# The output projection of a decoder block, as eight block products or as seven

## The chip, the cores and the metric

The kernel runs on one core of a Trainium2 chip. Such a core has several engines with instruction queues of their own: TensorE multiplies matrices (a weight load holds one operand still, the other streams through), VectorE and ScalarE do elementwise work, and GpSimd (POOL) and SyncE (SP) here mostly issue transfers. TensorE's results go to PSUM, eight banks of 512 float32 columns in 128 partitions. The metric is the device time of one execution in microseconds (us), as the median of several runs.

## The reference

The reference is one layer: two token mixers side by side, merged by gates, then an output projection, then an MLP with a squared ReLU. The sequence is 512 tokens, the width 1024, the MLP's inner width 4096, all in float32. What matters here is its end:

```
glu = g_s @ w_glu[l] + b_glu[l]
y_ssm = glu[..., :D_MODEL] * jax.nn.sigmoid(glu[..., D_MODEL:])

mixed = jax.nn.sigmoid(z_gla) * y_gla + jax.nn.sigmoid(z_ssm) * y_ssm
h = h + rmsnorm(mixed @ w_out[l], g_mix_post[l])

hn = rmsnorm(h, g_ffn_pre[l])
f = jnp.square(jax.nn.relu(hn @ w_ff1[l])) @ w_ff2[l]
h = h + rmsnorm(f, g_ffn_post[l])
```

`rmsnorm(x, g)` is x times the reciprocal root of the mean of its squares, times g.

## The kernel before

Every dense product is made in three passes. A float32 operand is split into a high half, rounded by a ScalarE copy to the reduced type that TensorE takes (`split_hi`, L160), and a low half, which VectorE makes by subtracting the high half (L175, L1428, L1444). The product is the sum of high x high, high x low and low x high, so one block of 128 x 128 weights against up to 512 columns costs three matmuls.

The stages that the change touches follow one another:

- The GLU (from L1398). Its 16 output tiles of 128 channels by 512 tokens are made in four groups of 256 channels: first the two sigmoid tiles of a group, then its two value tiles. A tile is 8 blocks x 3 passes = 24 matmuls. When a value tile is complete, VectorE adds the bias and multiplies by the gate (L1425), adds the other mixer's part (L1426) and the result, `mixed` in the reference, is split into `mh` and `ml`. The weights come over the SP queue into `wraw`, with three buffers.
- The output projection (`w_out_passes`, `h_rows`). All of w_out is loaded and split ahead, into `woh` and `wol`. Then the four tiles of 128 token rows follow one another, each with two banks of 512 output channels and 48 matmuls.
- The rows (`h_rows`). For each row tile: squares (ScalarE) and multiplication by `gpost`, a root (`row_scale`, a handful of operations on one column), addition of x (L1491), squares and multiplication by `gffn` (L1493), another root, and scaling to `hn` (L1496 on VectorE, L1497 on ScalarE). A row tile is then turned by eight TensorE transposes into two banks (L66), and one ScalarE and one VectorE operation per bank split it into `hh` and `hl`. The turn of row tiles 0 and 1 stands two row tiles after they are made, that of 2 and 3 among the first MLP tiles.
- The first MLP matrix (ff1). Three tiles (`EARLY`) first run on the columns of row tiles 0 and 1 alone, and later on the columns of 2 and 3. The others use all 512 columns at once.
- The second MLP matrix is already made as one level of Strassen's algorithm, from L1580 on, with its own sums of blocks.

TensorE's instructions keep their written order through these stages. VectorE's and ScalarE's are ordered by a planner, which goes by its own estimate of when an instruction could run and, among those that could, takes the one written first; `issue_after` queues a part behind a given instruction of the same engine. On the chip each engine then works off its queue in that order. A tile's tag has a number of buffers, and whoever wants the next one waits until it is free.

Of the kernel before, what the change touches and what calls it, by code (L numbers as in the profile page):

```python
# [10 lines left out]
F32R = mybir.dt.float32r  # L11
# [39 lines left out]
def hybrid_block(ctx: ExitStack, tc: tile.TileContext, io, out: bass.AP):  # L51
# [43 lines left out]
    def f32(t):  # L95
        return t.bitcast(F32)
# [26 lines left out]
    G.memset(sgn[:64], 1.0)  # L123
    G.memset(sgn[64:], -1.0)

    vecs = mk(cst, [P, 36], tag="vecs")
    V_GN, V_BGLU, V_BGATE, V_D = 0, 8, 24, 28

    def bank(tag="sm"):
        return mk(ps_mm if tag == "mm" else ps_sm, [P, 512], tag=tag)  # L130
# [28 lines left out]
    def split_hi(dst, src, scale=1.0):  # L159
        S.activation(dst, src, AF.Copy, scale=scale)  # L160
# [21 lines left out]
    def load_w(src):  # L182

        return [split_w(raw_w(src[:, c : c + P])[1]) for c in range(0, src.shape[1], P)]
# [1202 lines left out]
    s1.close()  # L1387


    sw = ExitStack()  # L1390
    pw = pool("pw", stack=sw, padded=True)
    mh = mk(pw, [P, KT, SEQ], F32R, tag="mh")
    ml = mk(pw, [P, KT, SEQ], F32R, tag="ml")
# [4 lines left out]
    for m in range(KT):  # L1398
        if m == NBLK - 1:
            q = blocks[m].qT  # L1400
        else:
            q = mk(pgl, [P, SEQ], tag="qi", bufs=4)
            nc.gpsimd.dma_start(q, qd[m])
        split_hi(gh[:, m], q)
        V.tensor_sub(gl[:, m], q, f32(gh)[:, m])
    wg = io["w_glu"][0]
    for c in range(0, D, 256):
        ss_ = []
        for i, w in enumerate(load_w(wg[:, D + c : D + c + 256])):
            m = c // P + i  # L1410
            ps = bank("mm")
            feat_tile(w, gh, gl, 0, SEQ, ps)
            s_ = mk(pgl, [P, SEQ], tag="ms", bufs=2)
            S.activation(s_, ps, AF.Sigmoid, bias=vecs[:, V_BGLU + 8 + m : V_BGLU + 9 + m])
            zt = mk(pgl, [P, SEQ], tag="zi", bufs=2)
            nc.sync.dma_start(zt, zs[m])
            V.tensor_mul(s_, s_, zt)
            ss_.append(s_)
        for i, w in enumerate(load_w(wg[:, c : c + 256])):
# [6 lines left out]
            V.tensor_add(ss_[i], ss_[i], t)  # L1426
            split_hi(mh[:, m], ss_[i])
            V.tensor_sub(ml[:, m], ss_[i], f32(mh)[:, m])  # L1428
    sgl.close()
    skept.close()  # L1430


    h_dram = mk(dr, [TT, P, D], tag="hd")
    gpost = mk(pw, [P, D], tag="gpost")
    gffn = mk(pw, [P, D], tag="gffn")
    nc.scalar.dma_start(gpost, io["g_mix_post"][0].partition_broadcast(P))
    nc.scalar.dma_start(gffn, io["g_ffn_pre"][0].partition_broadcast(P))
    woh = mk(pw, [P, KT, D], F32R, tag="woh")
    wol = mk(pw, [P, KT, D], F32R, tag="wol")
    for k in range(KT):  # L1440
        raw = mk(wp, [P, D], tag="wraw", bufs=3)
        nc.sync.dma_start(raw, io["w_out"][0][k * P : (k + 1) * P, :])
        split_hi(woh[:, k], raw)
        V.tensor_sub(wol[:, k], raw, f32(woh)[:, k])  # L1444

    def squares(pl, acc, i, src):
        junk = mk(pl, [P, 512], tag="junk", bufs=2)
        S.activation(junk, src, AF.Square, accum_out=acc[:, i : i + 1])

    def sums(pl, tag):  # L1450
        return mk(pl, [P, 2], tag=tag + "acc", bufs=2)

    def row_scale(pl, acc, tag):

# [10 lines left out]
    def w_out_passes(t, pss, order):  # L1465

        ts_ = slice(t * P, (t + 1) * P)
        for k, n in order:
            ns = slice(n * 512, (n + 1) * 512)
            PE.matmul(pss[n], mh[:, k, ts_], woh[:, k, ns], start=(k == 0), stop=False)  # L1470
            PE.matmul(pss[n], mh[:, k, ts_], wol[:, k, ns], start=False, stop=False)
            PE.matmul(pss[n], ml[:, k, ts_], woh[:, k, ns], start=False, stop=(k == KT - 1))
            yield

    def h_rows(t, pss):

        xt = mk(pt, [P, D], tag="xt", bufs=2)
        for i in range(2):
            nc.sync.dma_start(xt[i * CH : (i + 1) * CH], io["x"][0].rearrange("(c t) d -> t c d", t=T8)[2 * t + i])
        acc = sums(pt, "wo")  # L1480
        ht = mk(pt, [P, D], tag="ht", bufs=2)
        for n in range(2):
            ns = slice(n * 512, (n + 1) * 512)
            squares(pt, acc, n, pss[n])
            V.tensor_mul(ht[:, ns], pss[n], gpost[:, ns])
        rs = row_scale(pt, acc, "wo")
        hn = mk(pt, [P, D], tag="hn", bufs=2)
        acc = sums(pt, "hn")
        for n in range(2):
            ns = slice(n * 512, (n + 1) * 512)  # L1490
            V.scalar_tensor_tensor(ht[:, ns], ht[:, ns], rs, xt[:, ns], op0=ALU.mult, op1=ALU.add)  # L1491
            squares(pt, acc, n, ht[:, ns])
            V.tensor_mul(hn[:, ns], ht[:, ns], gffn[:, ns])  # L1493
        nc.gpsimd.dma_start(h_dram[t], ht)
        rs = row_scale(pt, acc, "hn")
        V.tensor_scalar(hn[:, :512], hn[:, :512], rs, None, op0=ALU.mult)  # L1496
        S.activation(hn[:, 512:], hn[:, 512:], AF.Copy, scale=rs)  # L1497
        return hn

    hns = []  # L1500
    for t in range(TT):
        pss = [bank("mm") for _ in range(2)]
        order = [(k, n) for n in range(2) for k in range(KT)]
        if t == 0:
            order = [(k, n) for k in range(KT) for n in range(2)]
        for i, _ in enumerate(w_out_passes(t, pss, order)):
            if i == 2 and t >= 2:
                transpose_tokens(hns[t - 2], P, hh, hl, (t - 2) * P, "sm")
        hns.append(h_rows(t, pss))

    EARLY = 3
    w1 = io["w_ff1"][0]
    w2 = io["w_ff2"][0]
    ws = load_w(w1[:, : EARLY * P])
    pss = [bank("mm") for _ in ws]
    for i, (w, ps) in enumerate(zip(ws, pss)):
        within = None
        if i == EARLY - 1:
            within = (4, lambda: transpose_tokens(hns[3], P, hh, hl, 3 * P, "sm"))
        feat_tile(w, hh, hl, 0, 256, ps[:, :256], within=within)  # L1520
        if i == 0:
            transpose_tokens(hns[2], P, hh, hl, 2 * P, "sm")
    spt.close()
    sw.close()
    pff = pool("pff", padded=True)
# [2 lines left out]


    NJ = MF // 2  # L1530
    HT = SEQ // 2
    s1 = mk(pff, [P, NJ, HT], tag="s1")
    td2 = mk(dr, [4, NJ, P, 512], tag="t2d")

# [32 lines left out]
    pinned[0] = False  # L1567
    for m, ps in enumerate(pss):
        relu2(m, ps)
    j = 0  # L1570
    for m in range(EARLY, MF):
        ps = bank("mm")
# [128 lines left out]
def laid_out(np, given):  # L1701

    a = {name: np.asarray(given[name]) for name in _INS + _LAID}
    ar, ai, br, bi, cr, ci = (a[name][0] for name in ("a_re", "a_im", "b_re", "b_im", "c_re", "c_im"))
    step = np.broadcast_to(a["log_step"][0], (64, 64))
    rows = {"vecs": np.concatenate([a[n][0].reshape(-1, P) for n in ("gla_norm_g", "b_glu", "b_gate", "d_skip")]).T}
# [12 lines left out]

_LAID = ["g_mix_pre", "w_gate_up", "gla_norm_g", "b_glu", "b_gate", "d_skip", "a_re", "a_im", "log_step", "b_re", "b_im", "c_re", "c_im"]  # L1720
_INS = [
    "x", "meta_tokens", "w_in", "w_o_gla", "w_glu", "w_out", "g_mix_post", "g_ffn_pre", "w_ff1", "w_ff2", "g_ffn_post",
]
_OUTS = [((1, SEQ, D), "float32")]

# [18 lines left out]
```

## Time and profile before

| what | us |
|---|---|
| median of three runs | 875.36 (875.29 to 875.64) |
| the profiled execution | 874.97 |
| its span in the profile | 873.2 |
| GLU, first matmul to last | 403.0 to 490.1 |
| output projection, first matmul to last | 490.1 to 535.4 |
| first passes of three ff1 tiles, with two turns | 535.4 to 545.8 |

A timeline's or chain's row gives the start, the duration, engine and line, the operation, the output and inputs by name, their shapes and the count; in brackets stands the idle time before it and who ended it. A group's row gives the count, total busy time and, behind the comma, the mean in nanoseconds, then the idle time. A row of a table of stretches gives its bounds and length, then busy time and count for TensorE, its weight loads, VectorE, ScalarE and POOL, then TensorE's granted clock, the transfer engines' share and GB/s.

### The profile page before, as it was taken

To read this page: it belongs to the slowest core of one execution; us is meant where nothing else is said; L and a number is where in the kernel's file an instruction comes from. 1 tells how busy PE (TensorE), PEld (TensorE's weight loads), DVE (VectorE), ACT (ScalarE), POOL (GpSimd) and SP (SyncE) were. 2 spreads that over 40 slices of the span, in tenths; PEclk is the share of its full clock that TensorE was granted. 3 is DMA by queue.
4 is the path that set the end of the run, shared out by engine and by line. 5 is a ranking of instruction groups with operands and counts; after the bars stand their busy time and mean duration, and the time that the engine had idled before them with its cause. 6 is when DMAs were issued, how large, how long until landed. Compare 5 with 4: busy or idle time off the path is not lost.

```text
span 873.2 us, 13275 instructions
## 1 busy us (share of the span) xinstructions
PE 862.7 (99%) x4824; PEld 738.3 (85%) x4824; DVE 654.6 (75%) x1181; ACT 442.4 (51%) x749; POOL 121.4 (14%) x213
## 2 busy tenths in 40 slices
PE   9999999999999999999999999999999999999996
PEld 8998889898988888888888889888888888888884
DVE  7999889979686699855446656576766677688886
ACT  7677456676763554334333544333222236665763
POOL 1123021130303222241000001011111100000001
PEclk9999999999999999999999999999999999999999
DMA  9777766545455747658545842498989966755464
GB/s 315 235 228 230 209 140 162 168 137 158 113 145 160 242 133 208 209 151 298 155 147 174 238 132 100 142 352 291 320 289 341 320 224 232 272 195 198 169 199 140
DMA packets 166905, 180.57 MB, mean 207 GB/s; under 512 B 18056, under 2 KB 126760, under 8 KB 166840
## 3 DMA queue, kind: packets, MB, share of 16 engines
q1 hardware_dynamic: 146832, 115.95, 44.6%
q0 software_dynamic: 17744, 58.52, 19.8%
q10 hardware_dynamic: 2264, 5.25, 1.9%
q8 instruction: 38, 0.62, 0.3%
q14 instruction: 27, 0.22, 0.1%
HBM read 143.74 MB, written 35.95 MB: 206 GB/s over the span
## 4 chain that ended last, share of the span: by engine, by line
PE 95%; DVE 3%; ACT 1%; issue 0%; ACTq 0%; DVEq 0%
PE mm L61 70%; PE sm L61 23%; PE sm L66 2%; DVE wlo L79 1%; DVE M L79 0%; DVE c L1665 0%; ACT whi L79 0%; DVE xT L79 0%; ACTq L79 0%; ACT vs L79 0%; DVE vs L79 0%; DVE c L1659 0%; DVE d L79 0%; DVE mta L79 0%; ACT L79 0%
## 5 line engine op out<-in xcount | busy, mean ns | idle before, releaser
L160 ACT ACTIVATE whi<-wraw 128x1024 fp32r<-128x1024 f32 x82 | 86.9, 1059 | 210.6 <-PE mm L61 191.8
L175 DVE TENSOR_TENSOR wlo<-wraw,whi 128x1024 fp32r<-128x1024 f32 x82 | 100.3, 1223 | 98.2 <-ACT whi L160 98.0
L61 PE MATMUL mm<-xh,whi 128*128 128x512 f32 (+2 forms) x464 | 158.9, 342 | 0.0
L61 PE MATMUL mm<-xh,wlo 128*128 128x512 f32 (+2 forms) x464 | 155.9, 336 | 0.0
L61 PE MATMUL mm<-xl,whi 128*128 128x512 f32 (+2 forms) x464 | 155.6, 335 | 0.0
L61 PE MATMUL mm<-hh,whi 128*128 128x512 f32 (+1 forms) x280 | 104.0, 371 | 0.0
L61 PE MATMUL mm<-hl,whi 128*128 128x512 f32 (+1 forms) x280 | 103.8, 371 | 0.0
L61 PE MATMUL mm<-hh,wlo 128*128 128x512 f32 (+1 forms) x280 | 103.8, 371 | 0.0
L61 PEld LDWEIGHTS mm<-xh,whi 128*128 128x128 f32 x464 | 87.6, 189 | 9.5 <-issue 1.0
L61 PEld LDWEIGHTS mm<-xh,wlo 128*128 128x128 f32 x464 | 87.5, 189 | 9.0
L61 PEld LDWEIGHTS mm<-xl,whi 128*128 128x128 f32 x464 | 87.6, 189 | 8.4
L1602 DVE TENSOR_TENSOR wlo<-wraw,whi 128x1024 fp32r<-128x1024 f32 x56 | 68.4, 1223 | 20.1 <-ACT whi L1598 20.1
L61 PE MATMUL sm<-wlo,fh 128*128 128x512 f32 x192 | 74.8, 390 | 0.0
L61 PE MATMUL sm<-whi,fl 128*128 128x512 f32 x192 | 74.7, 389 | 0.0
L61 PE MATMUL sm<-whi,fh 128*128 128x512 f32 x192 | 74.7, 389 | 0.0
L1598 ACT ACTIVATE whi<-wraw 128x1024 fp32r<-128x1024 f32 x56 | 58.6, 1049 | 16.8 <-PE mm L61 11.7
L61 PEld LDWEIGHTS mm<-hh,whi 128*128 128x128 f32 x280 | 52.8, 188 | 9.1
L61 PEld LDWEIGHTS mm<-hh,wlo 128*128 128x128 f32 x280 | 52.7, 188 | 9.0
L61 PEld LDWEIGHTS mm<-hl,whi 128*128 128x128 f32 x280 | 52.8, 188 | 9.0
L160 ACT ACTIVATE fh<-f 128x512 fp32r<-128x512 f32 x48 | 30.3, 631 | 45.5 <-PE sm L61 30.3
L61 PE MATMUL mm<-gh,whi 128*128 128x512 f32 x128 | 49.8, 389 | 0.0
L61 PE MATMUL mm<-gl,whi 128*128 128x512 f32 x128 | 49.8, 389 | 0.0
(445 smaller groups left out, 1787.6 us busy)
## 6 DMA issues: line engine op xcount, KB each, us to landing
wraw<-in_w_ff_dram SPq DMA_DIRECT2D x56, 512.0 KB, 4.7
wraw<-in_w_in_dram SPq DMA_DIRECT2D x46, 512.0 KB, 4.1
w2raw<-in_w_ff_dram POOLq DMA_DIRECT2D x16, 1024.0 KB, 8.6
t2d<-w2t POOLq DMA_DIRECT2D x16, 1024.0 KB, 5.7
wraw<-t2d SPq DMA_DIRECT2D x32, 512.0 KB, 3.9
wraw<-in_w_glu_dram SPq DMA_DIRECT2D x16, 512.0 KB, 4.3
M<-kpad POOLq DMA_DIRECT2D x64, 64.0 KB, 3.1
wraw<-in_w_o_gla_dram SPq DMA_DIRECT2D x8, 512.0 KB, 6.1
```

The costliest lines, as they stand in the source:

```text
L61: ins = nc.tensor.matmul(*args, **kw)
L66: ins = nc.tensor.transpose(*args, **kw)
L79: return lambda *args, **kw: tc.keep_in_program_order(getattr(self.engine, name)(*args, **kw))
L160: S.activation(dst, src, AF.Copy, scale=scale)
L175: V.tensor_sub(lo, raw, f32(hi))
L1598: halved = S.activation(bh, raw, AF.Copy)
L1602: V.tensor_sub(bl, raw, f32(bh))
```

## The change

The 1024 x 1024 matrix w_out and the mixed rows are cut into 2 x 2 blocks: tokens in halves of 256, output channels in halves of 512, and the inner channels by even and odd tiles of 128. Instead of eight block products there are seven (Winograd's form of Strassen's algorithm), each of two row tiles by 4 inner blocks by 3 passes, of certain sums of the blocks:

- `mixed` makes the four sums of the mixed rows' blocks and splits all seven operands, as soon as a GLU tile is complete. It takes the place of the split into `mh` and `ml`.
- `out_load` and `out_weights` load two row blocks of w_out (1 MB) from the POOL queue in each of the four GLU groups, make four sums, split three of the seven weight operands, and store the other three sums in DRAM from the POOL queue. The buffer `woraw` is one. In the last group `out_weights` is queued behind the gating of its sigmoid tiles, in the others behind the addition of the value tiles.
- `later_b` reloads the four other weight operands (three sums, one block) over SP and splits them during the products, into the buffers of three earlier ones.
- The results are gathered from three pairs of banks. Row tiles 0 and 1 are complete after the fifth product, 2 and 3 after the seventh; each row tile's halves are squared and multiplied as they come.
- The MLP norm's vector `g_ffn_pre` no longer multiplies the rows (L1493 goes). It lies along partitions in `vecs` and is applied at the turn (`turn_rows`): eight ScalarE and eight VectorE operations of 128 columns for a row tile instead of two and two.
- Row 0 is turned inside the seventh product, row 1 right behind it, rows 2 and 3 among the first ff1 tiles. `EARLY` becomes 4; the fourth tile's weights go into a buffer pair of the projection's.

```diff
+    def out_load(j):
+        raw = mk(pwo, [P, 2, D], tag="woraw", bufs=1)
+        nc.gpsimd.dma_start(raw, w_out[2 * j * P : (2 * j + 2) * P, :].rearrange("(k p) n -> p k n", p=P))
+        return raw
+    def out_weights(j, raw):
+        w11, w12, w21, w22 = (raw[:, k, n : n + 512] for k in range(2) for n in (0, 512))
+        t1, t2, t3, t4 = (mk(pgl, [P, SEQ], tag="qi", bufs=4) for _ in range(4))
+        V.tensor_sub(t1, w12, w11)
+        V.tensor_sub(t2, w22, t1)
+        V.tensor_sub(t3, w22, w12)
+        V.tensor_sub(t4, w21, t2)
+        for (hi, lo), src in ((b1, w11), (b2_, w21), (b5_, t1)):
+            split_to(hi[:, j], lo[:, j], src)
+        for i, t in enumerate((t2, t3, t4)):
+            nc.gpsimd.dma_start(tdo[i, j], t)
+    def mixed(c, i, src):
+        m = src.rearrange("p (h t) -> p h t", h=2)
+        if i == 0:
+            split_to(ah[A11][:, c], al[A11][:, c], m[:, 0])
+            return
+        e, o = mixed.even, m
+        split_to(ah[A12][:, c], al[A12][:, c], o[:, 0])
+        split_to(ah[A22][:, c], al[A22][:, c], o[:, 1])
+        V.tensor_add(o[:, 1], e[:, 1], o[:, 1])
+        V.tensor_sub(e[:, 1], e[:, 0], e[:, 1])
+        V.tensor_sub(e[:, 0], o[:, 1], e[:, 0])
+        V.tensor_sub(o[:, 0], o[:, 0], e[:, 0])
+        for n, part in ((S1, o[:, 1]), (S2, e[:, 0]), (S4, o[:, 0]), (S3, e[:, 1])):
+            split_to(ah[n][:, c], al[n][:, c], part)
...
-            V.tensor_mul(hn[:, ns], ht[:, ns], gffn[:, ns])
...
+    def out_product(acc, i, b, t, first=False):
+        ts_ = slice(t * P, (t + 1) * P)
+        for k in range(4):
+            for n, (x_, w_) in enumerate(((ah[i], b[0]), (ah[i], b[1]), (al[i], b[0]))):
+                PE.matmul(acc[t], x_[:, k, ts_], w_[:, k], start=first and k == 0 and n == 0, stop=k == 3 and n == 2, skip_group_check=True)
+    def later_b(src):
+        hi, lo = b_slot()
+        for jj in range(2):
+            raw = mk(wp, [P, 2, 512], tag="wraw", bufs=3)
+            nc.sync.dma_start(raw, src(jj))
+            later_b.made = split_to(hi[:, 2 * jj : 2 * jj + 2], lo[:, 2 * jj : 2 * jj + 2], raw)
+        return hi, lo
...
+    def turn_rows(t):
+        col = slice(t * P, (t + 1) * P)
+        for q in range(2):
+            pv = turned_tokens(hns[t], P, q, "sm")
+            for k in range(4):
+                kk = 4 * q + k
+                g = vecs[:, V_GF + kk : V_GF + kk + 1]
+                S.activation(hh[:, kk, col], pv[:, k], AF.Copy, scale=g)
+                V.scalar_tensor_tensor(hl[:, kk, col], pv[:, k], g, f32(hh)[:, kk, col], op0=ALU.mult, op1=ALU.subtract)
...
+    for t in range(2):
+        out_product(Xo, A11, b1, t, True)
...
+    b6 = later_b(sums_of(0))
+    for t in range(2):
+        out_product(Zo, A12, b2_, t, True)
+        V.tensor_add(rows_[t][:, sides[0]], rows_[t][:, sides[0]], Zo[t])
+        out_half(t, 0, 0)
+        rows_x(t)
+    b3 = later_b(w22_of)
+    ws = load_w(w1[:, : 3 * P])
...
+        out_product(Yo, S1, b5_, t, True)
...
+    b7 = later_b(sums_of(1))
...
+        out_product(Xo, S2, b6, t)
+        S.copy(rows_[t][:, sides[1]], Xo[t])
+    b4 = later_b(sums_of(2))
+    for t in range(2):
+        out_product(Yo, S4, b3, t)
+        with tc.issue_after(later_b.made.ins):
+            V.tensor_add(rows_[t][:, sides[1]], rows_[t][:, sides[1]], Yo[t])
+        out_half(t, 1, 1)
+        hns[t] = h_rows(t)
...
+        out_product(Xo, S3, b7, t)
+        with tc.issue_after(out_half.squared.ins):
+            S.copy(rows_[2 + t][:, sides[1]], Xo[t])
...
+    for t in range(2):
+        out_product(Xo, A22, b4, t)
+        turn_rows(t)
+        out_half(2 + t, 0, 1, Xo[t])
+        hns[2 + t] = h_rows(2 + t)
+    EARLY = 4
...
+    with tc.issue_after(second[0].ins), tc.issue_after(second[1].ins):
+        split_to(*kept_w, raw)
...
+        within = (6, lambda: turn_rows(3)) if i == 2 else None
         feat_tile(w, hh, hl, 0, 256, ps[:, :256], within=within)
+        if i == 1:
+            turn_rows(2)
```

More of the change, by code (lines that the diff above doesn't have):

```diff
@@ L1405, in hybrid_block, with split_to @@
         V.tensor_sub(gl[:, m], q, f32(gh)[:, m])
+    def split_to(hi, lo, src):
+        split_hi(hi, src)
+        return V.tensor_sub(lo, src, f32(hi))
+    def out_load(j):
[27 more added lines that the diff above has]
+            split_to(ah[n][:, c], al[n][:, c], part)
     wg = io["w_glu"][0]
-    for c in range(0, D, 256):
+    for c4, c in enumerate(range(0, D, 256)):
         ss_ = []
@@ L1425, in hybrid_block, with sums @@
             V.scalar_tensor_tensor(ss_[i], ps, vecs[:, V_BGLU + m : V_BGLU + m + 1], ss_[i], op0=ALU.add, op1=ALU.mult)
-            V.tensor_add(ss_[i], ss_[i], t)
-            split_hi(mh[:, m], ss_[i])
-            V.tensor_sub(ml[:, m], ss_[i], f32(mh)[:, m])
+            added = V.tensor_add(ss_[i], ss_[i], t)
+            mixed.even = ss_[0].rearrange("p (h t) -> p h t", h=2)
+            mixed(c4, i, ss_[i])
+        if c4 < 3:
+            with tc.issue_after(added.ins):
+                out_weights(c4, raw)
     sgl.close()
+    swo.close()
     skept.close()
     h_dram = mk(dr, [TT, P, D], tag="hd")
[L1434 to L1444, printed above, removed]
     def squares(pl, acc, i, src):
         junk = mk(pl, [P, 512], tag="junk", bufs=2)
-        S.activation(junk, src, AF.Square, accum_out=acc[:, i : i + 1])
-    def sums(pl, tag):
-        return mk(pl, [P, 2], tag=tag + "acc", bufs=2)
+        return S.activation(junk, src, AF.Square, accum_out=acc[:, i : i + 1])
+    def sums(pl, tag, bufs=2):
+        return mk(pl, [P, 2], tag=tag + "acc", bufs=bufs)
     def row_scale(pl, acc, tag):
@@ L1478, in h_rows, with row_tile, rows_x @@
+    sides = slice(0, 512), slice(512, D)
+    accs = [sums(pt, "wo", 4) for _ in range(TT)]
+    xts_ = {}
+    def row_tile():
+        return f32(mk(pw, [P, 4, HT], F32R, tag="aq", bufs=14)).rearrange("p a b -> p (a b)")
+    def rows_x(t):
+        xt = xts_[t] = mk(pt, [P, D], tag="xt", bufs=2)
         for i in range(2):
             nc.sync.dma_start(xt[i * CH : (i + 1) * CH], io["x"][0].rearrange("(c t) d -> t c d", t=T8)[2 * t + i])
-        acc = sums(pt, "wo")
-        ht = mk(pt, [P, D], tag="ht", bufs=2)
@@ L1482, in h_rows, with out_half @@
[L1482 to L1486, printed above, removed]
+    def out_half(t, n, i, src=None):
+        dst = rows_[t][:, sides[n]]
+        src = dst if src is None else src
+        out_half.squared = squares(pt, accs[t], i, src)
+        V.tensor_mul(dst, src, gpost[:, sides[n]])
+    def h_rows(t):
+        ht, xt = rows_[t], xts_[t]
+        rs = row_scale(pt, accs[t], "wo")
```

95 lines of the change are left out of this document (55 added, 40 removed).

## The prediction

> **What bounds the kernel now.** I read the page's busy shares first, then the chain that ended last, then TensorE's own waits, then the busy time of the two stretches that the change touches (GLU 397.70 to 490.08, output projection to 535.60).
>
> ```profile
> PE 862.7 (99%) x4824; PEld 738.3 (85%) x4824; DVE 654.6 (75%) x1181; ACT 442.4 (51%) x749; POOL 121.4 (14%) x213
> ...
> PE 95%; DVE 3%; ACT 1%; issue 0%; ACTq 0%; DVEq 0%
> ```
> ```profile
> 397.71 116.33 PE mm L61 x513
> ...
> 539.33 4.31 PE mm L61 x36
> 543.63 0.87 PE sm L66 x8
> 544.50 167.85 PE mm L61 x780
> ```
> ```profile
> PE sm L61 <- DVE xss L513: 1.3, 1, 1.3
> PE sm L61 <- DVE xrs L79: 0.5, 1, 0.5
> PE sm L61 <- DVE meta L79: 0.3, 1, 0.3
> ```
> ```profile
> 397.70:490.08 92.38, 92.38 (x409) 76.43 (x408) 51.94 (x63) 37.37 (x46) 2.25 (x5) 1.00 0.60 193
> 490.08:535.60 45.52, 45.52 (x211) 37.87 (x210) 27.32 (x71) 19.51 (x44) 1.62 (x3) 1.00 0.49 139
> ```
>
> TensorE carries 95% of the chain. In both stretches the TensorE column fills the stretch, the clock is 1.00, and the only waits of TensorE that the trace shows (2.1 us) lie in other stages. So a matmul removed there is worth its full pitch, until something that it waits for comes late. VectorE has 40.4 us spare of 92.4 in the GLU and 18.2 of 45.5 in the projection; ScalarE has more.
>
> **The matmuls.** The pitch of a 512-column matmul is 116.33/513 = 0.2268 us, of a 256-column one 4.31/36 = 0.1197 us (the 0.39 us that single rows show overlap).
>
> ```profile
> L61 PE MATMUL mm<-woh,mh 128*128 128x512 f32 x64 | 25.1, 392 | 0.0
> ...
> L61 PE MATMUL mm<-woh,ml 128*128 128x512 f32 x64 | 24.9, 389 | 0.0
> L61 PE MATMUL mm<-wol,mh 128*128 128x512 f32 x64 | 24.9, 389 | 0.0
> ```
>
> Before: 3 x 64 = 192. After: 7 products x 2 row tiles x 4 blocks x 3 passes = 168, of the same shape. 24 x 0.2268 = 5.44 us less. EARLY from 3 to 4 splits one more ff1 tile: 48 x 0.1197 - 24 x 0.2268 = +0.30. The 32 transposes stay. Ceiling of the gain: 5.14 us. [...]
>
> **VectorE and ScalarE in the GLU.** Each step below starts from these prices; successive starts give the cost to the queue: 0.60 us for 512 columns, 1.14 for 1024. 256 columns: 0.42 less the same overlap of 0.08, 0.34.
>
> ```profile
> L1444 DVE TENSOR_TENSOR wol<-wraw,woh 128x1024 fp32r<-128x1024 f32 x8 | 9.8, 1224 | 3.3 <-ACT woh L160 3.1
> ...
> L1428 DVE TENSOR_TENSOR ml<-ms,mh 128x512 fp32r<-128x512 f32 x8 | 5.5, 688 | 0.1
> ...
> L1493 DVE TENSOR_TENSOR hn<-ht,gffn 128x512 f32<-128x512 f32 x8 | 5.1, 684 | 0.0
> ...
> L235 DVE TENSOR_TENSOR mta<-E 128x256 f32<-128x256 f32 x7 | 3.0, 422 | 0.0
> ```
> ```profile
> L160 ACT ACTIVATE whi<-wraw 128x1024 fp32r<-128x1024 f32 x82 | 86.9, 1059 | 210.6 <-PE mm L61 191.8
> ...
> L1642 ACT COPY c<-sm 128x512 f32<-128x512 f32 x6 | 3.5, 581 | 0.8 <-PE sm L61 0.8
> ```
> ```profile
> 474.88 1.22 DVE L175 TENSOR_TENSOR wlo<-wraw,whi 128x1024 fp32r<-128x1024 f32 x1 [1.82 <-ACT whi L160]
> 476.02 0.69 DVE L1417 TENSOR_TENSOR ms<-ms,zi 128x512 f32<-128x512 f32 x1
> ...
> 562.69 0.69 DVE L1554 TENSOR_TENSOR w2t<-w2raw 128x512 f32<-128x512 f32 x1
> 563.29 0.68 DVE L1543 TENSOR_TENSOR s<-f 128x512 f32<-128x512 f32 x1
> ```
>
> Per group of 256 columns the change adds `out_weights` (4 sums and 3 low halves, 7 x 0.60 = 4.2 us) and `mixed` (4 sums and 7 low halves, 11 x 0.34 = 3.7) and drops two low halves (1.2): +6.7 us on a group's 21.8, where VectorE now works 12.3 on average (51.94/92.38). It fits, so 0; if it did not, the matmul behind it would wait for its weights' low half. `wol` (9.8) leaves, but `later_b` brings 8 halves of the same price.
>
> **Queues.** SP loses 8 loads of w_out and gets 8 in `later_b`, behind the sums' stores. The ScalarE queue's gffn load goes, and gpost's now waits for memory of the GLU's tiles, with the splits of A12 and b6 queued behind it; these have 5 us of room each, so 0. POOL gets 4 loads and 12 stores; it was idle 98.63 us there, so only their landing counts.
>
> ```profile
> 506.02 0.54 POOL L1494 DMA_DIRECT2D hd<-ht  x1 [98.63 <-DVE ht L1491]
> ```
> ```profile
> 469.31 0.69 DVE L1426 TENSOR_TENSOR ms<-ms,ti 128x512 f32<-128x512 f32 x1
> ...
> 482.67 0.69 DVE L1417 TENSOR_TENSOR ms<-ms,zi 128x512 f32<-128x512 f32 x1
> ```
> ```profile
> DMA to landing us min/median/max: 6.3/8.6/10.0
> ```
>
> The place to watch is the last load, because `woraw` has one buffer. Group 2's `out_weights` may start after the addition at 469.31, and shares VectorE with `mixed` (3.4) and a weight split (1.1), so it ends near 479. Only then is the last megabyte loaded; the row above is that of the 1 MB loads of w_ff2 from the same queue, so it lands at 485 to 489, 488 by the median. Four sums (2.4), the low half of b1 (0.6), and the last but one GLU tile's own work (1.6) then give 491 to 493; block 3 of the first product begins at 490.08 + 9 x 0.2268 = 492.1. Cost between 0 and 1.5 us; I take 0.2, since the median lands inside. [...]
>
> **The products in order.** From 490.08 each lasts 24 x 0.2268 = 5.44 us, so they end at 495.5, 501.0, 506.4, 511.9, 517.3, 522.7, 528.2. Each later weight block has a buffer free two products ahead of its use (10.9 us, against 1.1 + 2 x 1.2 = 3.5 for its split). A bank is always copied at least one half product (2.7 us) ahead of its next use, against 0.6 for the copy. VectorE between 483.3 and 515.6: two tiles 2.5, `mixed` 3.7, sums 4.2, 8 later halves 9.1, three ff1 weights 3.4, left halves 2.4, in all 25.3 of 32.3. It just fits; stalls here 0.
>
> **The rows.** The first product's rows 0 and 1 are complete only after product 5.
>
> ```profile
> 501.16 0.60 ACT L1448 ACTIVATE junk<-mm 128x512 f32<-128x512 f32 x1
> ...
> 502.04 1.28 ACT L143 ACT_TABLE_LOAD   x1 [0.18 <-DVE wo_r L140]
> ...
> 508.63 0.72 ACT L1497 ACTIVATE hn<-hn,hnrs 128x512 f32<-128x512 f32 x1 [1.09 <-DVE hnrs L147]
> ...
> 523.84 0.60 ACT L1448 ACTIVATE junk<-mm 128x512 f32<-128x512 f32 x1 [4.14 <-PE mm L61]
> ...
> 530.76 0.71 ACT L1497 ACTIVATE hn<-hn,hnrs 128x512 f32<-128x512 f32 x1
> ```
> ```profile
> 525.93 1.41 DVE L1491 SCALAR_TENSOR_TENSOR ht<-ht,wors,xt 128x512 f32<-128x512 f32 x2
> ...
> 530.40 0.49 DVE L1496 TENSOR_SCALAR hn<-hn,hnrs 128x512 f32<-128x512 f32 x1
> ```
> ```profile
> 523.00:536.00 13.00, 13.00 (x65) 10.95 (x64) 6.96 (x21) 5.26 (x14) 0.53 (x1) 1.00 0.10 40
> ```
>
> From bank to normed row is 8.2 us with the table load (501.16 to 509.35), 7.6 without (523.84 to 531.47). Row 0's bank is ready at 514.7, but its addition is queued behind b4's low halves, which can't be written before product 4 ends: 512.0 + 1.1 + 2 x 1.2 = 515.6. Add 0.7 and 8.2: 524.5, for a turn at 490.08 + 13 x 2.72 = 525.5. One microsecond of room. Row 1: 518.2 + 7.6 = 525.8 and 1.5 of row 0's work, for 529.1. Cost 0 to 2.0 (another row's work inserted); I take 0.5, because the room is positive.
>
> **The turns.** The matmuls of ff1 now follow row 1's turn directly; before, most of row 3's 48 matmuls lay between.
>
> ```profile
> 544.11 1.09 ACT L160 ACTIVATE hh<-sm 128x512 fp32r<-128x512 f32 x2 [1.20 <-PE sm L66]
> ```
> ```profile
> 544.74 1.29 DVE L213 TENSOR_TENSOR hl<-sm,hh 128x512 fp32r<-128x512 f32 x2 [2.07 <-ACT hh L160]
> ```
> ```profile
> L1156 DVE COPY_PREDICATED krow<-odd,sm 128x128 f32<-128x128 int32 x7 | 2.1, 296 | 0.0
> ```
> ```profile
> L1155 ACT COPY krow<-sm 128x128 f32<-128x128 f32 x7 | 1.8, 260 | 0.0
> ```
>
> Before, two operations on each engine turned a row; now eight of 128 columns with the vector in them, about 0.26 and 0.30 us by the nearest rows. A block of ff1 takes 3 x 0.12 = 0.36 us, so alone they keep up, after a start of 0.48 (543.63 to 544.11) + 0.26 + 0.30, where the 8 transposes cover 0.87: at least 0.3 us of wait. But row 2's addition of x (1.4), one root (some 0.5) and scaling (0.5), 2.4 us on VectorE, come in the same 2.9 us; if all of it goes first, the wait is 0.3 + 2.4 - (2.9 - 2.4) = 2.2. I take 1.1, the middle, as some of row 2's work waits for ScalarE anyway. Then rows 2 and 3 and the second passes: four rows of VectorE work cost 4 x (6.96 - 1.3 low halves - 1.3 gffn + 2.4 turn + 0.6 add) = 29.4, and the fourth ff1 weight 1.1, between 515.6 and about 546. Full, yet row 3 has 9.8 us to its turn against 7.6; cost 0 to 2.5, I take 0.3.
>
> **Sum.** -5.14 + 0.2 + 0.5 + 1.1 + 0.3 = -3.0 us. The profiled execution took 874.97 us (span 873.2); it becomes 872.0. The median of the runs stands 0.4 above that execution, so 872.3 for the median. A change of less than 0.2% (1.75 us) can't be told from none.
>
> **Rivals.** First, all waits are hidden: only the 0.3 of the first turn is left, 5.14 - 0.3 = 4.8 us, 870.5. For it: no wait of TensorE now; against it: VectorE has no spare time after 515.6.
> Second, the last w_out sums are late: landing after the row's maximum 10.0 and one more weight split (1.1) first, it is 479 + 10.0 + 1.1 + 4.6 = 494.7, 2.6 us late at the first product; with the other terms' 1.9 the waits are 4.5, so 874.7, no change that can be told. VectorE's queue, standing at a sum that waits for the load, holds back the last GLU tiles too. For it: one buffer. Against: the matmuls need these blocks last.
> Third, slower: the rows run one after another, because VectorE's order puts each row's end ahead of the next row's start. Row 0 ends at 523.8, row 1 at 531.4 (2.4 late), row 2 at 539.0, row 3 at 546.6, when its turn is due at 529.1 + 0.9 + 5.8 + 0.9 + 2.2 = 538.7: 7.9 us late, net 2.8 slower, 878.2. Speaking for it: 30.5 us of work in 30. Against: the rows overlap now. It decides once the waits exceed 5.14 + 1.75 = 6.9 us.
>
> **How the numbers follow.** Forecast 0.42, all hidden 0.20, late sums 0.15, rows in series 0.23. The first two are faster by over 0.2% (0.62), the third is no change (0.15), the last slower (0.23). The forecast's own range is 871.2 to 873.6. The whole range reaches from the ceiling of the gain, 870.2, to the serial rows, 878.2.
>
> **What will show it.** The projection's matmuls 168, 24 a product at 5.44 us; TensorE gaps, if any, at the first product's fourth block, at the turns of rows 0 and 1, in the first ff1 tile. A row of TensorE waiting on VectorE for `hl` of about 1 us is the forecast; on `bl` or `al` before 495, the second rival; on `hn` with several us, the third. A pitch other than 0.2268 would break the first term.

## The result, and the profile after

The changed kernel takes 889.72 us (888.63 to 890.8), the kernel before beside it 875.33: a ratio of 1.0165 with an interval from 1.0148 to 1.0183. It is slower, where 872.3 and a gain were forecast, and it lies outside the range. The profiled execution has a span of 887.3 us, 14.1 more than before.

The page's shares after: TensorE is about as busy as before. The chain that ended last now holds other engines and transfers; it is followed back only to 408.5, where TensorE waits for `gl`, so its 49% can't be set against the 95% before, which covers the whole span.

```profile
PE 865.2 (98%) x4824; PEld 738.5 (83%) x4824; DVE 685.1 (77%) x1267; ACT 464.4 (52%) x813; POOL 131.2 (15%) x229
...
PE 49%; DVE 2%; ACT 2%; DMA 1%; issue 0%; DVEq 0%; ACTq 0%
```

The busy time of TensorE does not tell that there is less matmul work, because a matmul is busy for longer where the granted clock is lower (in ff1's first tiles a 256-column row of the timeline lasts 0.41 us at a clock of 0.50 and 0.28 at 1.00). (Their count stays 4824: 24 go in the projection, and the fourth early tile is 24 matmuls cut in two.) What was lost shows in TensorE's waits after (us in total, times, longest):

```profile
PE mm L61 <- ACT aq L1620: 7.2, 1, 7.2
PE mm L61 <- DVE hl L1582: 1.5, 2, 1.0
PE mm L61 <- DVE gl L1419: 1.4, 2, 1.2
...
PE mm L61 <- DVE hn_r L140: 1.3, 1, 1.3
PE mm L61 <- ACT hh L1581: 1.0, 3, 0.4
```

Where they stand, from TensorE's timeline after:

```profile
408.53 0.50 PE L61 MATMUL mm<-gl,whi 128*128 128x512 f32 x1 [1.21 <-DVE gl L1419]
...
532.09 0.80 PE L61 MATMUL mm<-bh,aq 128*128 128x512 f32 x1 [7.21 <-ACT aq L1620]
...
540.76 1.03 PE L66 MATMUL sm<-ident,hn 128*128 128x128 f32 x8
...
545.67 0.39 PE L61 MATMUL mm<-hl,whi 128*128 128x256 f32 x1 [1.32 <-DVE hn_r L140]
...
563.16 0.28 PE L61 MATMUL mm<-hh,whi 128*128 128x256 f32 x1
```

And four stretches of after (the column before the last two is the granted clock): products 1 to 6; the first half of product 7; a piece of ff1's first tiles; and the twenty microseconds of the tail.

```profile
492.08:524.90 32.82, 32.80 (x145) 26.84 (x143) 21.74 (x33) 18.26 (x28) 0.00 (x0) 1.00 0.78 230
...
532.09:537.29 5.20, 5.20 (x14) 4.10 (x15) 4.23 (x15) 3.56 (x10) 0.54 (x1) 0.54 0.61 199
...
549.00:553.70 4.70, 4.70 (x23) 4.70 (x24) 3.72 (x15) 2.66 (x7) 0.53 (x1) 0.50 0.22 90
...
525.00:545.00 20.00, 10.87 (x44) 8.49 (x44) 16.67 (x55) 14.97 (x41) 1.08 (x2) 0.83 0.51 157
```

Product 7's first half has 12 matmuls; at the full pitch they take 2.72 us, here 5.20, at a clock of 0.54. The stretch in ff1's first tiles has a clock of 0.50 though TensorE was never idle in it. The time by stage, "due" being the count of matmuls and transposes by the pitches of the prediction (0.2268, 0.1197, 0.87 for a turn):

| stage | due, us | after, us | lost |
|---|---|---|---|
| GLU (before: 87.04) | 87.0 | 402.51 to 492.08, 89.6 | 2.5 |
| products 1 to 6, 144 matmuls | 32.7 | to 524.90, 32.8 | 0.2 |
| wait ahead of product 7 | 0 | to 532.09, 7.2 | 7.2 |
| product 7 and turns 0 and 1 | 7.2 | to 541.63, 9.5 | 2.4 |
| four ff1 first passes, turns 2 and 3 | 13.2 | to 563.16, 21.5 | 8.3 |

Lost in all 20.6; less the 5.14 us of matmuls that went, and 0.5 by which the GLU began earlier, 15.0. The span grew by 14.1, so 0.9 came back in later stages.

The 7.2 us are read from the chain after, in order of time (start, length, what):

```profile
497.68 5.44 PE sm L61 x24
503.12 5.45 PE mm L61 x24
...
509.19 0.97 ACT whi L160
510.18 1.24 DVE wlo L175
511.43 4.47 DMA wraw<-tdo
...
518.27 4.10 DMA wraw<-tdo
522.39 1.07 ACT bh L160
523.48 1.23 DVE bl L1423
524.71 0.61 DVE aq L1613
...
531.57 0.48 ACT aq L1620
532.09 5.20 PE mm L61 x12
```

The last load of `later_b` (b4's second half) lands at 522.4 and its low half is ready at 524.7. Only then comes row 0's addition (L1613), which is queued behind it, then row 0's and row 1's squares and roots, and behind row 1's squares the copies out of the banks (L1620) to which product 7 goes on adding. SyncE's queue and its waits after show why the load is so late:

```profile
490.68 0.36 SPq L1532 DMA_DIRECT2D wraw<-tdo  x1
491.14 0.44 SPq L1532 DMA_DIRECT2D wraw<-in_w_out_dram  x1
...
502.36 0.38 SPq L1532 DMA_DIRECT2D wraw<-in_w_out_dram  x1
503.49 5.64 SPq L166 DMA_DIRECT2D wraw<-in_w_ff_dram  x3
511.43 7.20 SPq L1532 DMA_DIRECT2D wraw<-tdo  x4
```
```profile
SPq L166 <- DVE bl L1423: 10.1, 6, 2.5
SPq L1532 <- DVE bl L1423: 9.7, 2, 7.5
SPq L1532 <- DVE wlo L175: 5.2, 3, 2.1
```

All these loads land in `wraw`, which has three buffers. A raw half keeps its buffer until it is split, and it cannot be split until the product that reads the old operand is over. So b3's second half waits to 502.36 for b6's split, ff1's three weight loads (L166), written between b3 and b7, take the buffers next, and the four halves of b7 and b4 start at 511.43, when ff1's first split gives one back.

### The profile page after: what moved, and what is told of

The parts are those of the page before. It is cut to its first block, busy times and chain, and to the rows that moved or that the text cites. A ratio compares the mean times of both kernels' runs of the same rounds, so it can differ in the third digit from the quotient of the medians.

```text
span 887.3 us, 13462 instructions
## 1 busy us (share of the span) xinstructions
PE 865.2 (98%) x4824; PEld 738.5 (83%) x4824; DVE 685.1 (77%) x1267; ACT 464.4 (52%) x813; POOL 131.2 (15%) x229
## 4 chain that ended last, share of the span: by engine, by line
PE 49%; DVE 2%; ACT 2%; DMA 1%; issue 0%; DVEq 0%; ACTq 0%
PE mm L61 34%; PE sm L61 15%; DMA wraw<-tdo 1%; ACT junk L1498 1%; DVE bl L1423 0%; ACT bh L160 0%; PE sm L66 0%; DVE hl L1582 0%; DVE c L1786 0%; DVE aq L1565 0%; DVE c L1780 0%; ACT L143 0%; DVE wlo L175 0%; ACT hh L1581 0%; ACT whi L160 0%
## 5 line engine op out<-in xcount | busy, mean ns | idle before, releaser
L61 PE MATMUL mm<-hh,wlo 128*128 128x512 f32 (+1 forms) x272 | 101.8, 374 | 0.0
```

What stands on the lines that cost most here:

```text
L61: ins = nc.tensor.matmul(*args, **kw)
```

## The experiments

Theory: the operands of the later products are late, because their loads share three buffers with ff1's weights, and the clock falls in the idle time that follows (0.54 in product 7's first half). Rivals: the two orders written out (addition behind b4, copies behind row 1's squares) are the cost themselves; or the turn in small pieces is. The GLU's loss is a matter of its own. Each experiment edits the changed kernel unless it says otherwise. Ratios are to the kernel before; line numbers move by one or two with the edits.

**ff1's weights ahead of the later blocks.** The load of ff1's first weights is moved from behind b3 to ahead of b6.

```diff
+    ws = load_w(w1[:, : 3 * P])
     b6 = later_b(sums_of(0))
...
     b3 = later_b(w22_of)
-    ws = load_w(w1[:, : 3 * P])
```

> The first try moved the three ff1 weights behind b4, and their splits (3 x 1.04 us on ScalarE, 3 x 1.2 on VectorE) then stood in the middle of row 0's own chain. Here they are requested ahead of the first late operand (b6) instead, so their splits fall into the end of the GLU. Staging theory: b7 and b4 find free buffers, b4's low half is ready near 517 to 518, the wait in front of the seventh product falls from 7.2 to below 1.5 us, no drop of the clock there; 879 to 881 us with the losses of the first ff1 tile left. Row theory: a wait of 4 us or more stays, here or at the turns of rows 0 and 1; 885 or more.

Measured: 881.2 us, 1.0066 (1.0051 to 1.0081), 8.5 less than the change. VectorE's timeline there: b4's last low half and row 0's addition come 5.5 us earlier than after, and the wait ahead of product 7 falls from 7.2 to 1.3.

```profile
517.98 1.23 DVE L1423 TENSOR_TENSOR bl<-wraw,bh 128x1024 fp32r<-128x1024 f32 x1 [0.45 <-ACT bh L160]
...
519.12 0.68 DVE L1613 TENSOR_TENSOR aq<-aq,mm 128x512 f32<-128x512 f32 x1
```
```profile
PE mm L61 <- ACT aq L1620: 1.3, 1, 1.3
```

The place of that one line is the largest part of the loss, with no operation added or removed.

**The same load behind b4.** The other way out of the row of loads.

```diff
-    ws = load_w(w1[:, : 3 * P])
...
     b4 = later_b(sums_of(2))
+    ws = load_w(w1[:, : 3 * P])
```

> The three ff1 weight tiles are requested after the projection's last weight operand (b4) instead of ahead of its last two (b7, b4); nothing else changes. Staging theory (the 7.21 us wait at the seventh product comes from b4's loads standing in three staging buffers behind the ff1 weights): b4's low half is ready near 517 instead of 524.7, row 0's addition follows then, the copy before the seventh product ends near 525, that wait falls below 1 us and the product runs at its 2.72 us per half instead of 5.2; 7.2 + 2.5 less, 880 us in all, with the losses of the first ff1 tile (8.3 us) left as they are. Row theory (four rows of work on VectorE and ScalarE can't be done in the time, whatever the loads do): the wait shrinks by less than 3 us, or comes back in front of the turn of row 0 or 1; 886 or more.

Measured: 888.26, 1.0145 (1.0129 to 1.0162). The wait ahead of product 7 fell to 4.2 us only. b4 came earlier, but ff1's splits, now last, stood inside row 0's chain on ScalarE and VectorE. The total is what the rival had foreseen (886 or more). Taken with the run before, it says that the sharing of `wraw` alone does not decide; what is last in it does.

**The two orders written out.** First the addition of row 0 and 1 is freed from b4, then instead the copies are freed from row 1's squares.

```diff
-        with tc.issue_after(later_b.made.ins):
-            V.tensor_add(rows_[t][:, sides[1]], rows_[t][:, sides[1]], Yo[t])
+        V.tensor_add(rows_[t][:, sides[1]], rows_[t][:, sides[1]], Yo[t])
```

> The order edge alone goes: the additions that complete rows 0 and 1 are no longer queued behind b4's low halves. b4's loads stay as late as they are. Staging theory with the edge as its carrier: row 0's addition starts near 517, the wait in front of the seventh product becomes that for b4 itself (its low half at about 524 to 526), 0 to 1.5 us instead of 7.2, no drop of the clock there; 879 to 881 us. If the edge carries nothing because VectorE's queue stands at b4's low halves anyway: wait 6 us or more, 888 us or more.

Measured: 883.48, 1.0094 (1.0069 to 1.0119), the wait 2.8 us, between the two readings. Row 0's addition now runs at 519.2, ahead of b4's last low halves, but these still stand on VectorE between the two halves of its addition of x.

```diff
-        with tc.issue_after(out_half.squared.ins):
-            S.copy(rows_[2 + t][:, sides[1]], Xo[t])
+        S.copy(rows_[2 + t][:, sides[1]], Xo[t])
```

> The order edge on the two copies out of the sixth product's banks goes, so they need not stand behind the squares of row 1 on ScalarE. The seventh product then starts as soon as b4 is there, near 525. Both theories say that rows 0 and 1 are still as late as before (row 0 normed at 533.5), so the wait moves to the turn of row 0: some 5 to 6 us there instead of 7.2 before the product; 885 to 889 us. If the copy alone was the cause, the wait goes for good: 878 to 881 us.

Measured: 886.78, 1.0123 (1.0106 to 1.014). Product 7 does not wait any more; TensorE waits in its middle instead, at row 0's turn:

```profile
534.15 1.97 PE L66 MATMUL sm<-ident,hn 128*128 128x128 f32 x8 [5.54 <-DVE hn L1569]
```

So the copy is mainly where the lateness showed. Both orders were then taken out of the kernel with ff1's weights early:

> As e5_w1_early, and both order edges (row additions behind b4, copies behind row 1's squares) are gone. If the edges only passed on b4's lateness, they cost nothing once b4 is early: within 1.5 us of e5_w1_early. If they have a price of their own (the copy stands behind row 1's squares whatever b4 does): 2 us or more below it.

Measured: 881.12, 1.0064 (1.0049 to 1.008), equal to 881.2. The orders carry b4's lateness to the rows; with b4 in time they cost nothing.

**TensorE kept busy in the wait.** 28 matmuls of 512 columns into a spare bank, ahead of product 7.

```diff
+    spare = bank()
+    for i in range(28):
+        PE.matmul(spare, ah[S3][:, i % 4, :P], b7[0][:, i % 4], start=i == 0, stop=i == 27, skip_group_check=True)
```

> 28 matmuls of 512 columns into a spare bank stand behind the sixth product (their result is read by nobody); 28 x 0.2268 = 6.35 us, which fits into the wait of 7.21. The wait for the copy stays, but TensorE is no longer idle. Clock theory (the seventh product's first half takes 5.20 us instead of 2.72 because the granted clock fell during the wait): this half takes 2.7 to 3.0 us, the granted clock between 525 and 538 stays near 1.00, 2.2 to 2.5 us less in all, 887 us. If the 5.20 us have another cause (the bank, the operands): 5 us again and 889 to 890 us.

Measured: 888.61, 1.0149 (1.0134 to 1.0165). TensorE's timeline there: product 7 starts at 534.15 and reaches row 0's transposes in 2.87 us, where it took 5.04 after (532.09 to 537.13).

```profile
534.15 0.50 PE L61 MATMUL mm<-bh,aq 128*128 128x512 f32 x1 [0.24 <-ACT aq L1620]
537.02 1.03 PE L66 MATMUL sm<-ident,hn 128*128 128x128 f32 x8
```

The granted clock is 1.00 from 534.10 to 539.50 there, where it was 0.54 from 532.09 to 537.29 in the change; so the half clock after the wait followed here from the idle time. But the 2.2 us hardly reached the total: row 1's turn and ff1's first matmuls now waited longer for the rows and their halves (0.5 us for `hn`, 1.4 for `hh`), and from product 7's start to ff1's first matmul it took 9.7 us against 10.1.

**The megabyte behind the last `qi` load.** In the GLU, the first load of w_out is queued behind the last load of `qi`.

```diff
-            nc.gpsimd.dma_start(q, qd[m])
+            loaded_q = nc.gpsimd.dma_start(q, qd[m])
...
-        with tc.issue_after(gated.ins):
+        with tc.issue_after(gated.ins), tc.issue_after(loaded_q.ins):
```

> Only the first megabyte of w_out is queued behind the loads that the GLU's operand is made from (same POOL queue). Queue theory for the waits of 1.4 us on the GLU's low operand (gl) and the 0.5 us around them: they go, the GLU takes 87.1 us again, and with them the drop of the clock that follows in some runs; 1.5 to 3 us less, 887 us. If those waits have another cause (ScalarE's splits of w_out at the same time): 1 us or more of waits on gl or gh stays, and 889 us.

Measured: 886.3, 1.0128 (1.0113 to 1.0143), 3.4 less than the change. POOL's queue after, and then in this experiment:

```profile
390.75 2.14 POOL L1417 DMA_DIRECT2D qi<-qd  x4
392.88 0.72 POOL L1427 DMA_DIRECT2D woraw<-in_w_out_dram  x1
398.03 0.60 POOL L1259 DMA_DIRECT2D td<-zt  x1 [4.43 <-DVE zt L1258]
398.62 1.60 POOL L1417 DMA_DIRECT2D qi<-qd  x3
```
```profile
397.25 0.54 POOL L1417 DMA_DIRECT2D qi<-qd  x1 [3.15 <-DVE gl L1419]
398.62 0.54 POOL L1417 DMA_DIRECT2D qi<-qd  x1 [0.83 <-DVE gl L1419]
399.22 0.54 POOL L1259 DMA_DIRECT2D td<-zt  x1
400.85 0.54 POOL L1417 DMA_DIRECT2D qi<-qd  x1 [1.09 <-DVE gl L1419]
401.47 0.72 POOL L1427 DMA_DIRECT2D woraw<-in_w_out_dram  x1
```

TensorE has no wait on `gl` left, between 400 and 420 it is busy for the whole 20.00 us, and the GLU takes 87.04 us again. Two things were against the `qi` loads in the change: the next of them is issued only behind `td`, which waited for VectorE until 398.03, where in this experiment two stand ahead of it; and they land after 6.1 us in the median, 4.9 in the kernel before. What each is worth, the transfer beside them or the order of the queue, this run does not separate.

**The vector back on the rows.** `gffn` multiplies the rows as before the change, and a turn has two operations on each engine.

```diff
+            V.tensor_mul(hn[:, sides[n]], ht[:, sides[n]], gffn[:, sides[n]])
...
-                S.activation(hh[:, kk, col], pv[:, k], AF.Copy, scale=g)
-                V.scalar_tensor_tensor(hl[:, kk, col], pv[:, k], g, f32(hh)[:, kk, col], op0=ALU.mult, op1=ALU.subtract)
+        transpose_tokens(hns[t], P, hh, hl, t * P, "sm")
```

> The MLP norm's vector multiplies the rows again (two VectorE operations of 512 columns for a row), and the turn is one ScalarE and one VectorE operation per bank again instead of eight of 128 columns each. Nothing else. If the many small operations of the turn cause the waits of the first ff1 tile (3.8 us of gaps and some 4 at half clock): gaps there below 2 us, 3 to 6 us less, 883 to 887 us. If row 2's and row 3's own work and the fourth ff1 weight's split between them cause the waits: 3 us of gaps or more stay, 888 to 891 us.

Measured: 888.25, 1.0145 (1.0117 to 1.0173). The listed gaps in ff1's first tile fall from 3.8 to 1.2 us, but row 3's turn waits 1.7 us for `hn` and row 1's 0.3. The total lies where the second reading had it (888 to 891), the gaps where the first had them. The moved vector trades one wait for another; it is not the cause.

**Both repairs together.** ff1's weights early, the megabyte behind `qi`, both orders taken out.

> Both repairs in one kernel: ff1's first weight load ahead of the first later block, out_load's first megabyte behind the last qi load, and the two orders written out around b4 and the copies removed. Theory (two separate losses that add): 881.1 less the 3.4 us that the qi order was worth alone = 877.7, between 876.5 and 879; no wait in the GLU, none before the seventh product, and the gaps in ff1's first tile with their half clock still there (2.6 us and about 2.7 us). Rival (the queue order in the GLU only shifts where the clock falls, and later work takes it up): 880 to 881.

Measured: 877.61, 1.0019 (1.001 to 1.0028). The two gains add: 12.1 of 14.4 us are back. What is left stands in ff1's first tile (waits there of 3.2 us) and its half clock (a mean of 0.70 from 535 to 540, 0.62 from 540 to 545).

**The tail of both repairs, reordered.** First, rows 2 and 3's last squares and norms, and the split of the kept weights, behind turn 1, and turns 2 and 3 one tile later. Second, instead, the vector back on the rows with the turns one tile later.

```diff
-        turn_rows(t)
-        out_half(2 + t, 0, 1, Xo[t])
-        hns[2 + t] = h_rows(2 + t)
+        turned = turn_rows(t)
+    with tc.issue_after(turned[0].ins), tc.issue_after(turned[1].ins):
+        for t in range(2):
+            out_half(2 + t, 0, 1, Xo[t])
+            hns[2 + t] = h_rows(2 + t)
...
-        within = (6, lambda: turn_rows(3)) if i == 2 else None
+        within = (4, lambda: turn_rows(3)) if i == 3 else None
...
-        if i == 1:
+        if i == 2:
             turn_rows(2)
```

> As the kernel with both repairs, and rows 2 and 3's last squares and norms and the split of the kept weights are ordered behind turn 1's last operations, and turns 2 and 3 come one tile later. Theory (the gaps in ff1's first tile come from row 2's operations and the kept split that stand between turn 1's eight pairs; the half clock comes from those gaps): the gaps fall from 2.6 us to under 1 us, no half clock at 540 to 545, 873 to 875.5, unless rows 2 and 3 come too late for their turns, which would show as waits on hn before turn 2 or 3. Rival (turn 1's sixteen small operations are themselves the limit: 8 pairs of about 0.35 us on each engine against 0.36 us of matmuls for each of the tile's first steps): gaps of 1.5 to 2.5 us stay, 876 to 878.

> As the kernel with both repairs, with the MLP norm's vector multiplied on the rows as in the kernel before (turns in two steps of 512 columns on each engine) and turns 2 and 3 one tile later, so that the 1.7 us that turn 3 waited has cover. Theory (first tile's loss is the moved vector's): gaps under 1 us and no half clock there, 873 to 875.5. Rival (the loss belongs to the late rows, whatever form the turn has): 876 to 878, with a wait on hn or hl in the turns.

Measured: 877.9, 1.0026 (1.0015 to 1.0037), and 877.19, 1.002 (1.001 to 1.003). Neither is better than both repairs. In the first the tile's gaps went (0.5 us left), and row 3 came 2.3 us late for its turn, row 1 0.5:

```profile
PE sm L66 <- DVE hn L1569: 2.9, 2, 2.3
```

**Gaps, clock or VectorE.** To both repairs are added: 15 matmuls between turn 1 and ff1's first tile; or the kept weights' split behind turn 1 and nothing else; or that and the first tile in two halves of 128 columns; or that and 10 matmuls.

```diff
+    for i in range(15):
+        PE.matmul(pss[0], ah[A22][:, i % 4, :P], b4[0][:, i % 4], start=i == 0, stop=i == 14, skip_group_check=True)
```
```diff
-    with tc.issue_after(second[0].ins), tc.issue_after(second[1].ins):
+    with tc.issue_after(turned[0].ins), tc.issue_after(turned[1].ins):
         split_to(*kept_w, raw)
```
```diff
+        if i == 0:
+            for c in (0, P):
+                feat_tile(w, hh, hl, c, c + P, ps[:, c : c + P])
```

> As the kernel with both repairs, with 15 matmuls of 512 columns between turn 1 and ff1's first tile, into the tile's own bank, which the tile then begins anew (nobody reads their result). By the 0.227 us between two such matmuls they take 3.4 us, about what the tile's gaps take. Theory (the half clock at 537.7 to 543.6, about 2.7 us, follows from the thin work of the tile's gaps): no half clock, no gaps over 0.5 us, 874.5 to 875.5. Rival (the clock falls for the whole stretch whatever TensorE does, or the gaps only move behind the added matmuls): 877 to 881.

> As the kernel with both repairs, with the split of the kept weights ordered behind turn 1's last operations. Theory (the split, 1.05 us on ScalarE at 531.09 and 1.21 us on VectorE at 535.95, stands inside turn 1 and is worth its time twice at most): 875.5 to 876.6. Rival (row 2's operations take the places that it leaves): 877 to 878.

> As the kernel with the kept split later, and ff1's first tile goes over columns 0 to 127 (row 0 alone) and then 128 to 255, so that TensorE has 24 matmuls to do that do not need turn 1. They cost 24 more matmuls of 128 columns; by the 0.1 us between the 128-column transposes that is 4.8 us for the tile in place of 2.9. Theory (turn 1 is what the tile waits for, and turn 0's halves are there): gaps under 1.5 us, no half clock, 873.5 to 875.5. Rival (turn 0's operations end no earlier than turn 1's, since they stand in the same queues): 877 to 879.

> Both repairs, the kept split behind turn 1, and 10 matmuls of 512 columns (2.3 us) between turn 1 and ff1's first tile, whose result nobody reads. Theory (two separate losses are left: gaps of about 2.3 us, which the ten matmuls replace, and a half clock at 535 to 540, which they prevent): 876.3 less 2 to 2.6 = 873.7 to 874.3, below the kernel before's 875.2. Rival (part of the half clock's loss is only waiting in another form, since turn 1's operations would be late for full-speed matmuls, as in the fill of fifteen, where 1.7 us of gaps stayed): 875 to 876.5, no better than the kernel before.

Measured: 876.87, 1.002 (1.0011 to 1.0029) with the fifteen; 876.27, 1.0013 (1.0004 to 1.0022) with the split later; 877.97, 1.0029 (1.0019 to 1.0039) with the halves; 876.08, 1.0009 (1.0 to 1.0019) with split and ten. Stretches of both repairs, then of the fifteen:

```profile
535.00:540.00 5.00, 3.22 (x14) 2.83 (x15) 4.96 (x19) 4.06 (x13) 0.53 (x1) 0.70 0.54 175
540.00:545.00 5.00, 5.00 (x30) 5.00 (x30) 3.04 (x11) 2.40 (x6) 0.53 (x1) 0.62 0.37 139
```
```profile
535.00:540.00 5.00, 3.33 (x21) 2.43 (x19) 4.96 (x19) 4.30 (x13) 0.53 (x1) 1.00 0.47 160
540.00:545.00 5.00, 5.00 (x41) 4.79 (x41) 3.63 (x12) 2.99 (x8) 0.53 (x1) 1.00 0.42 155
```

The fifteen keep the clock at 1.00, as expected, but gave at most 0.7 us of the 2.7 (by the medians; by the ratios, 1.002 against 1.0019, nothing): the matmuls that now run at full speed meet the same VectorE operations, and 1.7 us of waits on `hl`, `hh` and `hn_r` stay in the tile. The later split gave 1.3 us by the medians and some 0.5 by the ratios, whose intervals overlap, so its gain is not shown. The halves came out in their rival's range. The sum of fill and later split, 873.7 to 874.3 by the one theory, came out at 876.08, inside its rival's 875 to 876.5. What the tail meets is VectorE, by the waits that end with its `hl` (1.2 us with the fifteen, 1.3 with the split later). Its busy time in the 20 us from 525 on, before and with both repairs and the split later:

```profile
525.00:545.00 20.00, 20.00 (x133) 18.29 (x132) 12.94 (x40) 8.99 (x23) 2.50 (x4) 1.00 0.28 93
```
```profile
525.00:545.00 20.00, 17.67 (x99) 15.09 (x99) 17.75 (x63) 16.05 (x48) 1.61 (x3) 0.83 0.39 128
```

17.75 of 20 against 12.94. ScalarE's rose too, 16.05 against 8.99, and the two hand each other their operands. That VectorE's work there is the limit fits these runs; none took work off it, and none tells it from ScalarE's work or from the order of the two queues, so this last step is argued and not shown. Two things were not tried: staging buffers of their own for `later_b`, and a tail with fewer VectorE operations.

No version beats the kernel before. The best is 1.0009 with an interval that touches 1.

## Why the prediction was wrong

- **The matmuls.** Right: 168 in the projection, 24 a product in 5.44 us, products 1 to 6 in 32.82 us against 32.66. The ceiling of 5.14 us held as a price, and never became a gain.
- **VectorE in the GLU.** Right: it fits. VectorE was busy for 62.4 of the GLU's 89.6 us, against 47.8 of 87.1 before, and no matmul waited for a weight's low half.
- **Queues.** Wrong for POOL: "it was idle 98.63 us there, so only their landing counts". The same queue carries the `qi` loads at the GLU's start, and that idle time, which ended at 506.02, began only behind them, at 407.4. Priced at 0, the stage lost 2.5 in the profile (up to 5.9 in that of ff1's weights behind b4, where the clock fell too), and the order alone was worth 3.4 on the median.
- **The last load of w_out.** Right: it was issued at 480.1, landed near 486, inside the 485 to 489, and product 1 did not wait. The second rival did not occur.
- **"Each later weight block has a buffer free two products ahead of its use".** This is the step that failed. It looked at the buffers where the operands end, and counted SyncE's loads as eight for eight. The buffers where they land are three, shared with ff1's weights, and are held as long as the operand's own buffer is not free. Moving ff1's load gave back 8.5 us. The next sentence, that a bank is copied 2.7 us ahead of its next use, left out that the copies after product 6 are queued behind row 1's squares; there the 7.2 us showed.
- **The rows.** The order was read rightly: row 0's addition stands behind b4's low halves. Its date, 515.6, hung on the failed step; it was 524.7, 9.1 us later. The products had themselves begun 2.0 late, behind the GLU, so the "one microsecond of room" was some 6 us short. Priced at 0.5, it cost 7.2 and 2.4 of half clock.
- **The turns.** Mechanism right, size wrong: 1.1 us against 8.3. Of these 3.8 are waits of over 0.2 us in the first tile, 2.5 half clock (the chain has 38 matmuls in 7.02 us from 548.82 on, against 4.55 by the pitch), and the other 2.0 are shorter gaps and slower matmuls ahead of 548.82. Of the split of the kept weights the text had 1.1 us of VectorE in the whole tail, not that it stands between row 1's eight steps; what that cost is not clear of the noise (0.5 to 1.3 us).
- **Rows 2 and 3.** "Full" was right, but it was charged to the wrong place. At the turns of rows 2 and 3, priced at 0.3, TensorE did not wait in the change. Row 2's operations stand on VectorE between the eight steps of row 1's turn, so their cost falls into ff1's first tile: with both repairs and the split later the kernel is still about 6 us above the ceiling, 876.3 against 870.2.
- **The rivals.** The third, slower, was nearest: waits of several us at the rows, decided once they exceed 6.9. The cause was another, though: it put them down to VectorE's order of the rows; the operands' lateness, with the GLU's loss and the clock beside it, took it to 889.7.

No term stood for the clock. The prediction read 1.00 in both stretches and multiplied by a full pitch throughout.

## What to carry to other kernels

When loads are moved to just before their use, follow each one through the buffer that it lands in, and ask who holds that buffer and what that holder waits for: here free room at the destination did not help, and the place of one load in the row was worth 8.5 us. In a stretch in which TensorE was never idle before, price a new wait twice, once for itself and once for a fall of the clock behind it: here 7.2 us of wait, and 2.4 at a clock of 0.54. And read a queue's spare time in the stage where the new transfer is issued, against the transfers that stand there already.

## What the hardware showed

In the change the granted clock fell to 0.50 in a long wait, and once more where no wait was long. In the 7.2 us wait it was 1.00 until 530, some 5 us after the wait's start, then 0.50, and it stayed there to 536.8, 4.7 us into product 7. In ff1's first tile it was 0.50 again from 547.1 to 553.75, where no wait over 1.32 us had come before, only 5.5 us (541.63 to 547.1, at a clock of 1.00) in which TensorE was busy for 2.5; the pitch of the 256-column matmuls went from 0.120 to 0.213 us. With 28 matmuls put into the wait the clock was 1.00 from 534.10 to 539.50, and with fifteen ahead of ff1's first tile it was 1.00 from 535 to 545. With split and ten, in their profile, it was 0.72 from 535 to 540 and 0.59 from 540 to 545. What brings the fall where no wait is long, these runs do not show.

The same waits did not always bring it. Waits of 0.5, 0.2 and 1.2 us at the GLU's start left the clock between 400 and 420 at 1.00 in the run with row 0's addition freed, and at 0.83 in that of ff1's weights behind b4. With split and ten, nine executions with a mean clock of 0.996 to 0.998 took 875.0 to 877.0 us, three at 0.994 took 877.7 to 878.8.

The four 1 MB loads of w_out from POOL landed after 5.3 to 10.2 us, 5.9 in the median, in a GLU in which VectorE was busy for 62.4 of 89.6 us, and the first product, which needs the last of them, ran without a wait.
